# A Mamba-2 scan core rebuilt inside a hybrid encoder kernel: the step size goes into the exponent, the states come first

## The chip, the cores and the metric

The kernel runs on one core of a Trainium2 chip. The number compared is the device time of one execution in microseconds (us). Three runs of the kernel before took 1838.66, 1839.87 and 1843.01 us; their median, 1839.87 us, is the time that the prediction is for. Differences under 0.2% (3.7 us) count as no change.

The engines are TensorE (PE in the profile, with its weight loads as PEld), VectorE (DVE), ScalarE (ACT), GpSimd (POOL) and SyncE (SP, which issues the DMAs). Each engine works through its own list of instructions in a fixed order and waits at an instruction whose inputs or output buffer are not ready. The accumulators that PE writes lie in PSUM banks; everything else is in SBUF.

## The reference

Two layers on a sequence of 512 tokens of width 1024. Each layer normalises, projects, runs four groups of heads (a bidirectional Mamba-2 scan, a bidirectional RWKV-7 scan, differential attention, grouped-query attention), projects back and adds. The change lies in the first group alone:

```python
def _ssd(x, dt, A, bm, cm):                       # chunks of 128 tokens
    xdt = chunk(x * dt[..., None])
    a_cum = jnp.cumsum(dt * A, axis=-1)
    scores = einsum("bclhn,bcshn->bhcls", cm, bm) * exp(segsum(a))      # within a chunk
    y_diag = einsum("bhcls,bcshp->bclhp", scores, xdt)
    decay_states = exp(a_cum[..., -1:] - a_cum)
    states = einsum("bclhn,bclhp->bchpn", bm, xdt * decay_states)       # one per chunk
    ...                                                                 # carried from chunk to chunk
    y_off = einsum("bclhn,bchpn->bclhp", cm, states) * exp(a_cum)
    return y_diag + y_off
...
y = ssd(forward) + flip(ssd(backward)) + xs * d_skip
y = rms_norm_in_2_groups(y * silu(z))
```

There are 8 heads of 64 channels in 2 groups of 4; the state has 128 entries. Both directions are needed for every head.

## The kernel before

A layer has these stages: RWKV with the attention heads woven in, the Mamba-2 part (`ssd`), and the output projection (`mix` matmuls). Projections run as three matmuls for one product: each weight tile `wf` is split into a rounded part `whi` (ACT) and a rest `wlo` (POOL, or DVE for some output weights), so that every block of projection matmuls needs one ACT and one POOL instruction before it.

`ssd` first makes the step sizes (64 rows of 512 tokens: 8 heads forward, 8 heads backward at row 32) and their cumulative sums `ac` on DVE, with two exponentials and a logarithm on ACT. Three row tiles, `ac` (tile `se`), the step size `dt` (tile `sdt`) and the decay to the end of the chunk times the step size `dec` (tile `su`), are transposed on PE into `colT`, so that a token's value is a column usable as a per-partition scalar. `exT` is the exponential of the first.

Then it works through two groups g of four heads. For each head and direction a matmul `prow` spreads that head's cumulative sums over all partitions; DVE subtracts the column and takes the minimum with a mask `mneg` (four chunks, L811), ACT takes the exponential (L814). Two passes of DVE over both directions multiply by the step size and add (L819, L820), a third multiplies by the scores `gT` (L823), and PE makes `yd` from the result `mt` and the inputs `xs`; ACT moves `yd` into `y` for two heads at a time (L830). ACT also takes from each `prow` the decay of a whole chunk, `etot` (L807). After the four heads come the states: `xd` (POOL, L840), the matmul `stp`, the carried states `H` (POOL L847, DVE L850), the matmul `po` for the contribution of the carried states, `of` (DVE L861) and its addition to `y` (POOL L864), then the skip term `sk` (POOL L867) added by DVE (L869). At last `y` is gated with `zs` (L872), squared on ACT (`jk`), normalised into `zs` (L881), and later turned by PE (`ytr`) for the output projection.

Meanwhile PE is fed with other work. A filler holds generators of projection matmuls: for group 0 the projections of group 1 (96 `pjc` and 96 `pjt`, all of which must be out before group 1 starts), for group 1 the output projection's first half, which takes the contributions `kt` 4 to 15 in turn. Calls such as `fill(F_S3)` let it emit a set amount. Contributions 4 to 7 come from RWKV and are used as they are loaded; those from 8 on must first be transposed by PE (`ytr`) into a PSUM bank with the tag `pj`, of which there are two. The banks with the tag `g`, also two, serve `prow`, `yd`, `stp`, `po`, `pxt` and `pg`. After emission a list scheduler with a cost model of its own sets the order on each engine; it may move instructions ahead of others on the same engine.

Of the kernel before, what the change touches and what calls it, by code (L numbers as in the profile page):

```python
# [19 lines left out]
L = 512  # L20
# [55 lines left out]
def trunk(ctx: ExitStack, tc: tile.TileContext, x_in, win, wwd, wdt, wout, w2a, cols, rows, sscal, consts, out, dbg=None,  # L76
# [602 lines left out]
    def ssd(i, lay, ps, sp, op, yA, fill, more):  # L679
# [50 lines left out]
                            op=ALU.subtract)  # L730
        S.activation(dec, dec, AF.Exp)
        V.tensor_tensor(dec, dec, dt, op=ALU.mult)
        colT = sp.tile([128, 3, 4, 64], F32, tag="colT", name="colT")
        for n, src in enumerate((ac, dt, dec)):
            pcx = ps.tile([128, 4, 64], F32, tag="g", name="pcx")
# [55 lines left out]
        for g in range(2):  # L791
# [39 lines left out]

            H = [[None] * 4, [None] * 4]
            for step in range(3):
                stp = ps.tile([128, 2, 256], F32, tag="g", name="stp")
                for d in range(2):
                    ch = step if d == 0 else 3 - step
                    nx = ch + 1 if d == 0 else ch - 1
                    row = 32 * d + 4 * g
                    xd = sp.tile([128, 4, 64], F32, tag="xd", name="xd", bufs=2)
                    G.tensor_tensor(xd, xs[:, ch, :].rearrange("p (h v) -> p h v", h=4),  # L840
                                    colT[:, 2, ch, row:row + 4].unsqueeze(2).to_broadcast([128, 4, 64]), op=ALU.mult)
                    mm(stp[:, d, :], bt[:, ch, :], xd.rearrange("p h v -> p (h v)"), True, True)
                    hn = sp.tile([128, 256], F32, tag=f"H{d}{step}", name="H")
                    if step == 0:
                        V.tensor_copy(hn, stp[:, d, :])
                    else:
                        G.tensor_tensor(hn.rearrange("p (h v) -> p h v", h=4),  # L847
                                        H[d][ch].rearrange("p (h v) -> p h v", h=4),
                                        etot[:, d, ch, :].unsqueeze(2).to_broadcast([128, 4, 64]), op=ALU.mult)
                        V.tensor_tensor(hn, hn, stp[:, d, :], op=ALU.add)  # L850
                    H[d][nx] = hn
                fill(F_S3)
            for ch in range(4):
                po = ps.tile([128, 2, 256], F32, tag="g", name="po")
                ds = [d for d in range(2) if H[d][ch] is not None]
                for d in ds:
                    mm(po[:, d, :], cv[6 + g][:, ch * 128:ch * 128 + 128], H[d][ch], True, True)
                of = sp.tile([128, 2, 256], F32, tag="of", name="of", bufs=2)
                for d in ds:
                    row = 32 * d + 4 * g  # L860
                    V.tensor_tensor(of[:, d, :].rearrange("p (h v) -> p h v", h=4),  # L861
                                    po[:, d, :].rearrange("p (h v) -> p h v", h=4),
                                    exT[:, ch, row:row + 4].unsqueeze(2).to_broadcast([128, 4, 64]), op=ALU.mult)
                    G.tensor_tensor(y[:, ch, :], y[:, ch, :], of[:, d, :], op=ALU.add)  # L864
                fill(F_S4)
                sk = sp.tile([128, 256], F32, tag="sk", name="sk", bufs=2)
# [464 lines left out]
def _consts():  # L1331
# [17 lines left out]
    c[:, C_MNEG + 128:C_MNEG + 256] = np.where(p[:, None] >= p[None, :], 0.0, -1e30)  # L1349
# [102 lines left out]
```

## Time and profile before

| | |
|---|---|
| profiled execution | 1827.76 us, of it span 1826.0 us |
| PE busy | 1596.3 us (87%) |
| PEld busy | 1321.8 us (72%) |
| DVE busy | 1088.5 us (60%) |
| ACT busy | 826.5 us (45%) |
| POOL busy | 695.9 us (38%) |
| mean granted TensorE clock | 0.929 of full speed |
| `ssd` of the first layer, from its first matmul to the end of `y` | about 676 to 845 us |
| `ssd` of the second layer | about 1583 to 1754 us |

A row of the timeline gives the start, the duration, the engine, the line, what is written and read, and in brackets how long the engine had stood idle and what released it. A matmul's duration overlaps that of the next; what PE can do is read from the distance of starts.

### The profile page before, as it was taken

What the parts mean: (1) busy time and instruction counts of PE and PEld (TensorE: products, weight loads), DVE (VectorE), ACT (ScalarE), POOL (GpSimd) and SP (SyncE); (2) the same over time, 40 slices, a digit from 0 to 9 for tenths busy, and PEclk for the clock granted to TensorE, in tenths of its full rate; (3) what the DMA queues carried; (4) which work ended last, traced back from release to release, by engine and by line L of the source; (5) the groups of instructions that cost most, each with busy time, mean ns of one, the idle gap of its engine ahead of it and who ended that gap; (6) DMA issues with size and microseconds to landing.
All of it is one profiled execution on the core that took longest, in us unless ns stands there. A gap on an engine that the chain in (4) does not pass through costs nothing. (4 is left out here: it accounts for less than half of the span.)

```text
span 1826.0 us, 36868 instructions
## 1 busy us (share of the span) xinstructions
PE 1596.3 (87%) x15232; PEld 1321.8 (72%) x15232; DVE 1088.5 (60%) x2130; ACT 826.5 (45%) x1602; POOL 695.9 (38%) x708
## 2 busy tenths in 40 slices
PE   6888889879899898988887998898788989989888
PEld 6677767757788776766775787677567777768666
DVE  3577576575555437885245865755755554288852
ACT  4645336417345335543346453454272453454431
POOL 4543234242424234543455422343333332245333
PEclk9889989989999998999998899899898999989899
DMA  4110001011101014122321100111110110131223
GB/s 148 64 50 32 29 33 59 14 67 35 42 19 62 28 53 138 59 94 81 127 99 54 53 20 29 34 59 36 44 42 31 36 58 22 54 130 53 87 86 116
DMA packets 57512, 108.50 MB, mean 59 GB/s; under 512 B 6784, under 2 KB 8704, under 8 KB 57344
## 3 DMA queue, kind: packets, MB, share of 16 engines
q1 hardware_dynamic: 57344, 106.15, 17.4%
q8 instruction: 119, 1.95, 0.4%
q14 instruction: 49, 0.40, 0.1%
HBM read 95.64 MB, written 10.49 MB: 58 GB/s over the span
## 5 line engine op out<-in xcount | busy, mean ns | idle before, releaser
L145 POOL TENSOR_TENSOR wlo<-wf,whi 128x512 fp32r<-128x512 f32 x228 | 319.6, 1408 | 423.8 <-ACT whi L144 391.3
L82 PE MATMUL pjt<-whi,hhi 128*128 128x256 f32 x960 | 291.3, 303 | 3.7 <-ACT raw L270 1.7
L82 PE MATMUL pjt<-wlo,hhi 128*128 128x256 f32 x960 | 284.5, 297 | 0.8 <-POOL wlo L145 0.8
L82 PE MATMUL pjt<-whi,hlo 128*128 128x256 f32 x960 | 285.2, 297 | 0.0
L144 ACT ACTIVATE whi<-wf 128x512 fp32r<-128x512 f32 x228 | 142.1, 627 | 226.3 <-PE pjt L82 122.6
L82 PEld LDWEIGHTS pjt<-whi,hhi 128*128 128x128 f32 x960 | 191.8, 200 | 15.6 <-issue 7.3
L82 PEld LDWEIGHTS pjt<-whi,hlo 128*128 128x128 f32 x960 | 191.9, 200 | 6.1 <-issue 5.0
L82 PEld LDWEIGHTS pjt<-wlo,hhi 128*128 128x128 f32 x960 | 191.2, 199 | 5.2 <-issue 3.3
L82 PE MATMUL pjc<-hhi,whi 128*128 128x512 f32 x384 | 160.0, 417 | 16.9 <-ACT craw L751 10.7
L82 PE MATMUL pjc<-hhi,wlo 128*128 128x512 f32 x384 | 157.4, 410 | 3.5 <-POOL wlo L145 3.5
L82 PE MATMUL pjc<-hlo,whi 128*128 128x512 f32 x384 | 156.5, 407 | 0.0
L82 PE MATMUL mix<-whi,ylo 128*128 128x512 f32 x256 | 105.8, 413 | 5.5 <-DVE ylo L1234 5.5
L892 ACT ACTIVATE p<-sc,nm 128x512 f32<-128x512 f32 x96 | 65.6, 685 | 89.0 <-DVE nm L889 81.8
L82 PE MATMUL mix<-wlo,yhi 128*128 128x512 f32 x256 | 103.7, 405 | 0.0
L82 PEld LDWEIGHTS pjc<-hhi,whi 128*128 128x128 f32 x384 | 75.0, 195 | 39.5 <-ACT craw L751 12.4
L82 PE MATMUL mix<-whi,yhi 128*128 128x512 f32 x256 | 99.8, 412 | 4.0 <-ACT yhi L1233 4.0
L889 DVE TENSOR_REDUCE nm<-sc 128x1 f32<-128x512 f32 x96 | 64.5, 689 | 63.2 <-PE sc L82 63.1
L82 PE MATMUL pa<-AR,BK 64*64 64x128 f32 x1024 | 66.3, 341 | 37.7 <-DVE AT L450 37.5
L82 PEld LDWEIGHTS pjc<-hhi,wlo 128*128 128x128 f32 x384 | 75.2, 196 | 23.3 <-POOL wlo L145 5.6
L82 PE MATMUL sc<-qT,qT 64*128 64x512 f32 (+1 forms) x256 | 86.4, 478 | 3.8 <-ACT y L1050 1.8
L82 PEld LDWEIGHTS pa<-AR,BK 64*64 64x64 f32 x1024 | 52.8, 171 | 48.7 <-DVE AT L450 42.4
L82 PEld LDWEIGHTS pjc<-hlo,whi 128*128 128x128 f32 x384 | 75.6, 197 | 15.0 <-issue 0.7
(360 smaller groups left out, 3645.4 us busy)
## 6 DMA issues: line engine op xcount, KB each, us to landing
wf<-in_win_dram SPq DMA_DIRECT2D x224, 256.0 KB, 3.0
wf<-in_wout_dram SPq DMA_DIRECT2D x64, 256.0 KB, 2.7
y<-y_dram SPq DMA_DIRECT2D x24, 256.0 KB, 3.4
xt<-in_x_dram SPq DMA_DIRECT2D x8, 512.0 KB, 4.2
y_dram<-y SPq DMA_DIRECT2D x16, 256.0 KB, 3.3
y_dram<-rs SPq DMA_DIRECT2D x8, 256.0 KB, 2.8
x_dram<-t SPq DMA_DIRECT2D x8, 256.0 KB, 2.1
xt<-x_dram SPq DMA_DIRECT2D x4, 512.0 KB, 4.0
```

The costliest lines, as they stand in the source:

```text
L82: PE.matmul(o, lhsT, rhs, start=start, stop=stop, skip_group_check=skip)
L144: S.activation(hi, wf, AF.Copy)
L145: G.tensor_tensor(lo, wf, hi.bitcast(F32), op=ALU.subtract)
L889: V.tensor_reduce(nm, sc, axis=AX, op=ALU.max, negate=True)
L892: S.activation(p, sc, AF.Exp, bias=nm, accum_out=sm)
```

## The change

The step size is no longer a factor on the 128x128 blocks. Its logarithm is taken once per layer in the row layout (after a maximum with 1e-37) and subtracted from the cumulative sum, so that the transposed column already holds both; the minimum with the mask and the exponential then give decay times step size at once. The mask now holds +1e30 where the block is kept. The decays of whole chunks come from one small matmul `pe` per layer instead of 16 small exponentials. In each group the states and the skip term come first: POOL writes the skip term straight into `y`, adds the carried part to it, and only then the four heads follow, whose `yd` is added to `y` by DVE from the bank. For group 1 `yd` lies in a bank with the tag `pj`.

```diff
         V.tensor_tensor(dec, dec, dt, op=ALU.mult)
+        V.tensor_scalar(dt, dt, 1e-37, None, op0=ALU.max)
+        S.activation(dt, dt, AF.Ln)
+        V.tensor_tensor(dt, ac, dt, op=ALU.subtract)
         colT = sp.tile([128, 3, 4, 64], F32, tag="colT", name="colT")
...
+        ends = sp.tile([128, 4, 16], F32, tag="ends", name="ends")
+        for d in range(2):
+            V.tensor_tensor(ends[:, :, 8 * d:8 * d + 8], ac4[:, :, 127 * (1 - d):128 - 127 * d].to_broadcast([128, 4, 8]),
+                            selE.bitcast(F32)[:, 8 * d:8 * d + 8].unsqueeze(1).to_broadcast([128, 4, 8]), op=ALU.mult)
+        pe = ps.tile([128, 4, 16], F32, tag="g", name="pe")
+        mm(pe, one.to_broadcast([128, 128]), ends, True, True)
+        S.activation(etot, pe, AF.Exp)
+        V.tensor_scalar(dh, rws[:, R_D:R_D + 8], 0.5, None, op0=ALU.mult)
...
+            H = [[None] * 4, [None] * 4]          # states: moved ahead of the heads, text as before
+            for step in range(3):
...
+            for ch in range(4):
+                for d in ds:
+                    mm(po[:, d, :], cv[6 + g][:, ch * 128:ch * 128 + 128], H[d][ch], True, True)
+                G.tensor_tensor(heads(y[:, ch, :]), heads(xs[:, ch, :]),
+                                dh[:, 4 * g:4 * g + 4].unsqueeze(2).to_broadcast([128, 4, 64]), op=ALU.mult)
+                of = sp.tile([128, 2, 256], F32, tag="of", name="of", bufs=2)
+                for d in ds:
+                    row = 32 * d + 4 * g
+                    V.tensor_tensor(heads(of[:, d, :]), heads(po[:, d, :]),
+                                    exT[:, ch, row:row + 4].unsqueeze(2).to_broadcast([128, 4, 64]), op=ALU.mult)
+                    G.tensor_tensor(y[:, ch, :], y[:, ch, :], of[:, d, :], op=ALU.add)
+                fill(F_S4)
             for h in range(4):
                 for d in range(2):
                     mm(pr, selE[:, ri:ri + 1].to_broadcast([128, 128]), acs, True, True)
-                    S.activation(etot[:, d, :, h:h + 1], p4[:, :, 127:128] if d == 0 else p4[:, :, 0:1], AF.Exp)
                     for ch in range(4):
-                        V.scalar_tensor_tensor(ar[:, ch, :], p4[:, ch, :], colT[:, 0, ch, row:row + 1],
+                        V.scalar_tensor_tensor(ar[:, ch, :], p4[:, ch, :], colT[:, 1, ch, row:row + 1],
                                                mneg[:, d * 128:d * 128 + 128],
                                                op0=ALU.subtract, op1=ALU.min)
                     S.activation(ar, ar, AF.Exp)
-                for ch in range(4):
-                    V.tensor_scalar(ex[0][:, ch, :], ex[0][:, ch, :], colT[:, 1, ch, row:row + 1], None, op0=ALU.mult)
-                    V.scalar_tensor_tensor(ex[1][:, ch, :], ex[1][:, ch, :], colT[:, 1, ch, row + 32:row + 33],
-                                           ex[0][:, ch, :], op0=ALU.mult, op1=ALU.add)
-                V.tensor_tensor(mt, ex[1], gT, op=ALU.mult)
+                V.tensor_tensor(mt, ex[0], ex[1], op=ALU.add)
+                V.tensor_tensor(mt, mt, gT, op=ALU.mult)
                 if h % 2 == 0:
-                    yd = ps.tile([128, 4, 2, 64], F32, tag="g", name="yd")
+                    yd = ps.tile([128, 4, 2, 64], F32, tag="pj" if g else "g", name="yd")
                 if h % 2 == 1:
-                    S.activation(y[:, :, (h - 1) * 64:(h + 1) * 64], yd.rearrange("p c h v -> p c (h v)"), AF.Copy)
+                    V.tensor_tensor(yh, yd.rearrange("p c h v -> p c (h v)"), yh, op=ALU.add)
...
-                G.tensor_tensor(sk.rearrange("p (h v) -> p h v", h=4), xs[:, ch, :].rearrange("p (h v) -> p h v", h=4),
-                                rws[:, R_D + 4 * g:R_D + 4 * g + 4].unsqueeze(2).to_broadcast([128, 4, 64]), op=ALU.mult)
-                V.scalar_tensor_tensor(y[:, ch, :], sk, 0.5, y[:, ch, :], op0=ALU.mult, op1=ALU.add)
...
-    c[:, C_MNEG:C_MNEG + 128] = np.where(p[:, None] <= p[None, :], 0.0, -1e30)
+    c[:, C_MNEG:C_MNEG + 128] = np.where(p[:, None] <= p[None, :], 1e30, -1e30)
```

The order on the engines changes in the Mamba-2 part of both layers only. Three places of it, in the first layer:

ACT, where the columns `colT` are made, before (`su` is the decay row, `craw` empties a projection bank of PE):

```order
L731 ACTIVATE su<-su 64x512
L1233 ACTIVATE yhi<-y 128x512
L144 ACTIVATE whi<-wf 128x512
L738 ACTIVATE colT<-pcx 128x256
L144 ACTIVATE whi<-wf 128x512
L758 ACTIVATE cv<-cacc 128x512
L751 ACTIVATE craw<-pjc 128x512
```

and now:

```order
L731 ACTIVATE su<-su 64x512
L1244 ACTIVATE yhi<-y 128x512
L144 ACTIVATE whi<-wf 128x512
L735 ACT_TABLE_LOAD
L735 ACTIVATE sdt<-sdt 64x512
L775 ACT_TABLE_LOAD
L775 ACTIVATE cv<-cacc 128x512
L742 ACTIVATE colT<-pcx 128x256 x2
L768 ACTIVATE craw<-pjc 128x512
```

The logarithm with a table load on either side now stands ahead of `craw`, one `colT` has moved behind it, and one `whi` has gone from ahead of `craw` to a place further down.

POOL, at the start of group 0, before (`xd` feeds the states, `sk` is the skip term):

```order
L145 TENSOR_TENSOR wlo<-wf,whi 128x512 x2
L840 TENSOR_TENSOR xd<-xs,colT 128x256 x2
L867 TENSOR_TENSOR sk<-xs,srow 128x256 x2
L145 TENSOR_TENSOR wlo<-wf,whi 128x512 x7
L749 MEMSET craw 128x2
L750 MEMSET craw 128x2
L145 TENSOR_TENSOR wlo<-wf,whi 128x512
L840 TENSOR_TENSOR xd<-xs,colT 128x256
L847 TENSOR_TENSOR H<-H,etot 128x256
```

and now:

```order
L145 TENSOR_TENSOR wlo<-wf,whi 128x512 x2
L824 TENSOR_TENSOR xd<-xs,colT 128x256 x2
L843 TENSOR_TENSOR y<-xs,dh 128x256 x4
L824 TENSOR_TENSOR xd<-xs,colT 128x256
L832 TENSOR_TENSOR H<-H,etot 128x256
L824 TENSOR_TENSOR xd<-xs,colT 128x256 x2
L832 TENSOR_TENSOR H<-H,etot 128x256 x2
L824 TENSOR_TENSOR xd<-xs,colT 128x256
L832 TENSOR_TENSOR H<-H,etot 128x256
L145 TENSOR_TENSOR wlo<-wf,whi 128x512
L850 TENSOR_TENSOR y<-y,of 128x256 x6
L145 TENSOR_TENSOR wlo<-wf,whi 128x512 x4
```

The chain of the states, which was spread behind the weight splits of the heads, is now one block at the start of the group, with the four skip products inside it.

PE, in group 1 around the second head's `yd`, before:

```order
L82 MATMUL yd<-xs,mt 128x64 x4
L82 MATMUL mix<-wlo,yhi 128x512
L82 MATMUL mix<-whi,ylo 128x512
L82 MATMUL mix<-wlo,yhi 128x512
L82 MATMUL mix<-whi,ylo 128x512
L82 MATMUL prow<-acs,cr 128x512
L82 MATMUL mix<-wlo,yhi 128x512
```

(12 more `mix`, 8 `ytr` and 3 `mix` follow before the third head's `yd`), and now:

```order
L82 MATMUL mix<-whi,ylo 128x512
L82 MATMUL mix<-wlo,yhi 128x512
L82 MATMUL yd<-xs,mt 128x64 x4
L82 MATMUL prow<-acs,cr 128x512 x2
L82 MATMUL yd<-xs,mt 128x64 x4
L1239 MATMUL ytr<-cst,y 128x128 x4
L82 MATMUL mix<-whi,yhi 128x512 x4
```

Between the second and the third head's `yd` there is now no `mix`: 48 of them, which is four contributions, stand ahead of it, and the first `ytr` stands behind the third `yd`.

## Rows read from the trace of the kernel before

**Rows 1.** The page, part 1: busy time (share) xinstructions of PE.

```profile
PE 1596.3 (87%) x15232; PEld 1321.8 (72%) x15232; DVE 1088.5 (60%) x2130; ACT 826.5 (45%) x1602; POOL 695.9 (38%) x708
```

**Rows 2.** Busy time by stretch: length, engines, granted clock, DMA share, GB/s.

```profile
697.00:734.00 37.00, 30.72 (x178) 25.75 (x178) 31.93 (x35) 21.54 (x38) 20.20 (x22) 0.86 0.43 145
734.00:796.00 62.00, 53.32 (x293) 44.38 (x292) 53.30 (x116) 26.90 (x57) 34.65 (x39) 0.97 0.18 57
796.00:842.00 46.00, 43.58 (x217) 34.27 (x215) 35.76 (x99) 17.87 (x37) 16.44 (x21) 1.00 0.28 86
842.00:866.00 24.00, 20.52 (x82) 15.69 (x81) 13.22 (x20) 9.83 (x26) 5.66 (x5) 0.86 0.32 110
1641.00:1703.00 62.00, 53.36 (x288) 44.43 (x287) 52.81 (x114) 26.71 (x57) 34.28 (x38) 0.93 0.17 55
1749.00:1775.00 26.00, 20.44 (x90) 15.73 (x88) 14.22 (x22) 10.16 (x26) 7.03 (x7) 0.93 0.32 102
```

**Rows 3.** Waits of PE, 697 to 734: total, times, longest.

```profile
PE pjc L82 <- ACT craw L751: 4.3, 1, 4.3
```

**Rows 4.** Waits of PE, 734 to 796, group 0 of the first layer.

```profile
PE pxt L777 <- ACT xs L778: 5.1, 1, 5.1
PE pg L82 <- DVE cv L759: 1.3, 1, 1.3
```

**Rows 5.** Waits of PE, 842 to 866, behind group 1 of the first layer.

```profile
PE mix L82 <- DVE ylo L1234: 2.8, 1, 2.8
```

**Rows 6.** Groups of DVE instructions, 734 to 796: busy, mean ns, idle before.

```profile
L811 DVE SCALAR_TENSOR_TENSOR ar<-prow,colT,mneg 128x128 f32<-128x128 f32 x32 | 8.9, 343 | 4.6 <-ACT etot L807 4.6
L820 DVE SCALAR_TENSOR_TENSOR ar<-ar,colT 128x128 f32<-128x128 f32 x16 | 5.9, 431 | 0.2 <-ACT ar L814 0.2
L819 DVE TENSOR_SCALAR ar<-ar,colT 128x128 f32<-128x128 f32 x16 | 5.5, 399 | 0.8 <-ACT ar L814 0.8
L869 DVE SCALAR_TENSOR_TENSOR y<-sk,y 128x256 f32<-128x256 f32 x4 | 4.2, 1060 | 2.1 <-POOL y L864 2.1
L823 DVE TENSOR_TENSOR mt<-ar,gT 128x512 f32<-128x512 f32 x4 | 2.7, 684 | 0.0
```

**Rows 7.** Groups of PE instructions, 734 to 796.

```profile
L82 PE MATMUL stp<-xd,bt 128*128 128x256 f32 x12 | 3.7, 405 | 0.8 <-POOL xd L840 0.7
L82 PE MATMUL po<-H,cv 128*128 128x256 f32 x12 | 3.0, 389 | 0.0
```

**Rows 8.** Tile colT: duration ns min/median/max, first and last start.

```profile
L840 POOL TENSOR_TENSOR xd<-xs,colT x24: 606/613/1058, 733.1 to 1741.0; 128x256 f32<-128x256 f32 x24
```

**Rows 9.** Tile H.

```profile
L847 POOL TENSOR_TENSOR H<-H,etot x16: 612/988/1059, 767.2 to 1741.9; 128x256 f32<-128x256 f32 x16
```

**Rows 10.** Tile y.

```profile
L872 DVE SCALAR_TENSOR_TENSOR y<-y,zs x4: 1212/1220/1225, 786.4 to 1752.7; 128x1024 f32<-128x1024 f32 x4
```

**Rows 11.** Timeline of PE, 790 to 797.

```profile
790.96 1.11 PE L777 MATMUL pxt<-cst,cv 128*128 128x128 f32 x4 [5.09 <-ACT xs L778]
...
795.05 1.13 PE L82 MATMUL pg<-cv 128*128 128x128 f32 x8 [1.27 <-DVE cv L759]
...
796.25 0.39 PE L82 MATMUL mix<-wlo,yhi 128*128 128x512 f32 x1
796.48 0.39 PE L82 MATMUL mix<-whi,yhi 128*128 128x512 f32 x1
```

**Rows 12.** Timeline of ACT, 695 to 719.

```profile
695.85 1.28 ACT L707 ACT_TABLE_LOAD   x1
697.14 0.63 ACT L707 ACTIVATE sl<-su 64x512 f32<-64x512 f32 x1
...
718.10 0.60 ACT L751 ACTIVATE craw<-pjc 128x512 f32<-128x512 f32 x1 [0.22 <-PE pjc L82]
```

**Rows 13.** Groups of DVE instructions, 703 to 734.

```profile
L723 DVE TENSOR_SCALAR sdt<-sdt 64x512 f32<-64x512 f32 x1 | 1.3, 1317 | 0.0
L732 DVE TENSOR_TENSOR su<-su,sdt 64x512 f32<-64x512 f32 x1 | 0.7, 675 | 0.0
```

More of the change, by code (lines that the diff above doesn't have):

```diff
@@ L740, in ssd @@
         S.activation(exT, colT[:, 0], AF.Exp)
+        ends = sp.tile([128, 4, 16], F32, tag="ends", name="ends")
+        ac4 = acs.bitcast(F32).rearrange("p (c t) -> p c t", c=4)
+        for d in range(2):
[3 more added lines that the diff above has]
+        mm(pe, one.to_broadcast([128, 128]), ends, True, True)
+        etot = sp.tile([128, 4, 16], F32, tag="etot", name="etot")
+        S.activation(etot, pe, AF.Exp)
+        dh = sp.tile([128, 8], F32, tag="dh", name="dh")
+        V.tensor_scalar(dh, rws[:, R_D:R_D + 8], 0.5, None, op0=ALU.mult)
         gr = [{}, {}]
@@ L795, in ssd @@
             cv, zs, xs, bt, gT = (gr[g][n] for n in ("cv", "zs", "xs", "bt", "gT"))
-            etot = sp.tile([128, 2, 4, 4], F32, tag="etot", name="etot")
+            heads = lambda t: t.rearrange("p (h v) -> p h v", h=4)
             y = sp.tile([128, 4, 256], F32, tag="y", name="y")
+            H = [[None] * 4, [None] * 4]
+            for step in range(3):
+                stp = ps.tile([128, 2, 256], F32, tag="g", name="stp")
+                for d in range(2):
+                    ch = step if d == 0 else 3 - step
+                    nx = ch + 1 if d == 0 else ch - 1
+                    row = 32 * d + 4 * g
+                    xd = sp.tile([128, 4, 64], F32, tag="xd", name="xd", bufs=2)
+                    G.tensor_tensor(xd, heads(xs[:, ch, :]),
+                                    colT[:, 2, ch, row:row + 4].unsqueeze(2).to_broadcast([128, 4, 64]), op=ALU.mult)
+                    mm(stp[:, d, :], bt[:, ch, :], xd.rearrange("p h v -> p (h v)"), True, True)
+                    hn = sp.tile([128, 256], F32, tag=f"H{d}{step}", name="H")
+                    if step == 0:
+                        V.tensor_copy(hn, stp[:, d, :])
+                    else:
+                        er = 8 * d + 4 * g
+                        G.tensor_tensor(heads(hn), heads(H[d][ch]),
+                                        etot[:, ch, er:er + 4].unsqueeze(2).to_broadcast([128, 4, 64]), op=ALU.mult)
+                        V.tensor_tensor(hn, hn, stp[:, d, :], op=ALU.add)
+                    H[d][nx] = hn
+                fill(F_S3)
@@ new lines, in ssd @@
+            for ch in range(4):
+                po = ps.tile([128, 2, 256], F32, tag="g", name="po")
+                ds = [d for d in range(2) if H[d][ch] is not None]
+                for d in ds:
[4 more added lines that the diff above has]
+                for d in ds:
+                    row = 32 * d + 4 * g
+                    V.tensor_tensor(heads(of[:, d, :]), heads(po[:, d, :]),
+                                    exT[:, ch, row:row + 4].unsqueeze(2).to_broadcast([128, 4, 64]), op=ALU.mult)
+                    G.tensor_tensor(y[:, ch, :], y[:, ch, :], of[:, d, :], op=ALU.add)
+                fill(F_S4)
@@ L829, in ssd @@
                 if h % 2 == 1:
-                    S.activation(y[:, :, (h - 1) * 64:(h + 1) * 64], yd.rearrange("p c h v -> p c (h v)"), AF.Copy)
[L832 to L866, printed above, removed]
-                G.tensor_tensor(sk.rearrange("p (h v) -> p h v", h=4), xs[:, ch, :].rearrange("p (h v) -> p h v", h=4),
-                                rws[:, R_D + 4 * g:R_D + 4 * g + 4].unsqueeze(2).to_broadcast([128, 4, 64]), op=ALU.mult)
-                V.scalar_tensor_tensor(y[:, ch, :], sk, 0.5, y[:, ch, :], op0=ALU.mult, op1=ALU.add)
@@ L870, in ssd @@
+                    yh = y[:, :, (h - 1) * 64:(h + 1) * 64]
+                    V.tensor_tensor(yh, yd.rearrange("p c h v -> p c (h v)"), yh, op=ALU.add)
             tap("ssdy", y, lambda a: a[:, g * 256:g * 256 + 256].rearrange("(c p) v -> p c v", p=128))
@@ L1347, in _consts @@
     c[:, C_I64:C_I64 + 64] = (s[:, None] == np.arange(64)[None, :])
-    c[:, C_MNEG:C_MNEG + 128] = np.where(p[:, None] <= p[None, :], 0.0, -1e30)
-    c[:, C_MNEG + 128:C_MNEG + 256] = np.where(p[:, None] >= p[None, :], 0.0, -1e30)
+    c[:, C_MNEG:C_MNEG + 128] = np.where(p[:, None] <= p[None, :], 1e30, -1e30)
+    c[:, C_MNEG + 128:C_MNEG + 256] = np.where(p[:, None] >= p[None, :], 1e30, -1e30)
     n = np.arange(512)
```

1 line of the change is left out of this document (removed).

## The prediction

> **What bounds the kernel now.** I read the busy times first: PE is busy 87% of the span, and no other engine comes near [rows 1]. The three-way projection matmuls stay as they are, so the change can only win where PE stands idle. Next come the stretches [rows 2]. PE's idle time is length less busy time: in the first layer 8.7 us of the 62 us of group 0 (734 to 796), 2.4 us of the 46 us of group 1, and 3.5 us of the 24 us behind it; in the second layer 8.6 us for group 0 and 5.6 us behind group 1 (its group 1 repeats the first layer's). Then the waits. In group 0 most of the idle time is one wait of 5.1 us, of `pxt` for ACT's copy `xs`, and 1.3 us of `pg` for DVE [rows 4]. Neither is DVE's arithmetic on the heads: ACT's list has the four squares `jk` ahead of that copy, and these wait until `y` is finished, which takes the states, `po` and the skip term behind the last head. Behind group 1 PE waits 2.8 us for a `ylo` that stands on DVE behind the same kind of `y` [rows 5]. Ahead of the groups it waits 4.3 us for `craw` [rows 3].
>
> Idle time has a second price. A mean granted clock of 0.97 over 62 us is 3.7 us at the half level (1.2 GHz), 0.93 is 8.7 us, 0.86 over 24 us is 6.7 us [rows 2]. It falls behind such long waits. Half of what is left of it after the waits that fall into it is lost: (3.7 - 1.3) / 2 = 1.2 us in group 0 of the first layer, 3.2 us in the second (some 2.3 us of waits taken off), 2.3 us behind group 1 in the first, 1.2 us in the second.
>
> **The change part by part.** *DVE.* Per head and layer, four L819 (0.399 us) and four L820 (0.431 us) go and one whole-tile add comes, taken as L823 (0.684 us): 4 x 0.83 - 0.68 = 2.6 us less; over eight heads 21 us per layer by this stretch. The `sk` additions go (8 x 1.06 us), four additions of `yd` come (0.68 each, from ACT, which had them as copies) [rows 6]. None of this counts by itself: in group 0 DVE was busy 53.3 of 62 us, but so was PE [rows 2], and PE's waits there for `mt` are small change. It counts only as far as it shortens the end of `y`.
>
> *Preamble (+0.8 us a layer).* Ahead of `craw`, which began at 718.10, ACT now has the logarithm and two table loads of 1.28 us [rows 12]; on DVE come a maximum (bounds: nothing if it falls into an idle moment, 1.32 us as L723) and a subtraction (0.68 us as L732) [rows 13], and two tiny products. Following ACT's list from the end of `su`: the logarithm ends some 3.5 us later, `cv` and two `colT` follow, and `craw` starts at about 719. PE meanwhile has 35 `pjc` with no transposes between them and has moved four `pxt` forward, so that it reaches the first `pjt` 0 to 0.5 us late; `pe` costs 0.15 us and the next `whi` about 0.3 us. I take 0.8 us, between 0 and 2.6 us (both loads on PE's path).
>
> The trace prices the load at 1.28 us, and the logarithm behind it starts 0.01 us after its end [rows 12]. The Trainium skill (ScalarE: Activation LUTs, What ACT_TABLE_LOAD costs) adds a drain of about 1.38 us to each switch, 2.66 us in all. By that rule the preamble would be about 2.8 us dearer per layer.
>
> *States first (new waits).* In the new POOL order each group has two `xd`, four skip products, then `xd` and `H` alternating: 14 instructions from the first `xd` to the last `H`. At 0.61 us [rows 8, 9] that is 8.5 us plus one DVE addition, 9.0 us. PE has in that time six `stp` and six `po` (at most 3.7 + 3.0 us busy for both [rows 7], nearer 4.5 us by distance of starts) and 13 projection matmuls at 0.23 us [rows 11], 3.0 us, of which the `po` mostly come after the chain. `stp` number 3 waits for the xd behind the four skip products (2.3 us), the three after it 0.6, 0.35 and 0.65 us: 3.9 us in group 0. In group 1 POOL starts earlier against PE, since `pg` comes later than `xs`: 1.85 us. Before, this cost 0.7 us, as other work lay between. `H` has a median of 0.99 us and `xd` a maximum of 1.06 us [rows 8, 9]; at means of 0.71 and 1.02 us the chain would be 11.2 us, 2.7 us more in each of the four groups. I take 0.61, the median of `xd`, because only PSUM-reading DVE work lies beside the chain now.
>
> The Trainium skill (SBUF — State Buffer, Who interferes with whom) says that a DVE instruction with two SBUF inputs shuts out a GpSimd one that reads SBUF, and that one with at most one SBUF input does not. The spread of `xd` from 0.606 to 1.058 us agrees with it [rows 8]; by that rule the chain runs at 0.61.
>
> *End of group 0.* After the last head there are now one addition (0.68), the gating of 1.22 us [rows 10] and four squares, about 4.5 us, against 46 `pjt` (5.5 us) that PE still has: the 5.1 us wait goes. `pg` still waits for DVE, which has the four `zs` ahead of `cv`: 1.4 us. So group 0: before 8.7 + half clock 1.2 (second layer 8.6 + 3.2); now 3.9 + 1.4 + 1.2 for a fall of the clock behind the states: **-3.4 and -5.3 us**.
>
> *Group 1.* DVE needs per head eight `ar` (8.9 / 4 = 2.2 us), the tail of an exponential (0.6, as `craw`) and two whole-tile passes (1.4): 4.2 us [rows 6, 12]. PE has filler for it until 48 `mix` are used up; the next contribution needs a transpose into a `pj` bank, and `yd` holds one of the two until DVE has added it, the other being taken by the second `yd`. In the new order PE has two `prow` (0.5 us) between the second and third `yd`, against DVE's 4.2 us, of which 0.3 us are done by then: 3.4 us idle, plus 0.65 us for the first `yhi`. With the states' 1.85 us that is 5.9 us, and half clock 1.7 us; before 2.4 us: **+5.2 us** a layer.
>
> *Behind group 1.* `y` ends 2.5 us after the last `yd`, with transposes of two contributions and 24 `mix` at hand; 1.2 us of waits remain. Before: 3.5 + 2.3 and 5.6 + 1.2 us: **-4.6 and -5.6 us**.
>
> Sum: first layer 0.8 - 3.4 + 5.2 - 4.6 = -2.0; second 0.8 - 5.3 + 5.2 - 5.6 = -4.9; together -6.9 us. I take 6, since some of the idle time before is gaps too short to be listed, which will stay. The profiled execution (1827.76 us: 1826.0 and 1.76 around it) would become 1822. It lies 12.1 us under the median of the runs, and I carry the difference over: 1839.9 - 6 = **1834 us**.
>
> **Rivals.** (1) *The state chain on POOL becomes the bound, and the kernel is slower.* Place: the start of each group. Price: at the means of this stretch, 4 x 2.7 = 10.8 us more, and PE's clock falls longer: -6 + 10.8 + 2 gives +7, 1847 us. It cancels the gain at a mean of 0.72 us per instruction and costs 0.2% from 0.78 us. For it: `H` had 0.99 us in the median [rows 9]. Against: that was with two-input DVE passes beside it, which have left this place. Chance 0.22.
> (2) *The preamble eats the gain: no change.* If each of the two loads holds ACT twice its 1.28 us, `craw` comes 2.6 us later, PE stands at the bank, and 2 x 2.6 = 5 us are lost: 1839 us. For it: PE waited 4.3 us for just this copy, and a half clock followed [rows 2, 3]. Against: the load's row ends where the next begins [rows 12]. It is the place where the drain of the ScalarE page would show. Chance 0.17.
> (3) *More gain.* If PE's weights and banks let it take other work between the second and third `yd`, so that group 1 costs about what it did, 2 x 4.5 of its 2 x 5.2 us fall away: -6 - 9 gives 1825 us. For it: DVE has 4 x 2.6 + 4 x 1.06 - 2 x 0.68 = 13 us less in each group. Against: the order is fixed, and nothing ready stands there. Chance 0.13.
>
> **The numbers.** Forecast 0.48, with its own range 1828 to 1840. Range over all: 1823 to 1848. A change under 0.2% (3.7 us, so 1836.2 to 1843.5) can't be told from none. Faster: 0.40 of the forecast's 0.48 and all of (3), 0.53. Same: 0.08 of the forecast and (2), 0.25. Slower: (1), 0.22.
>
> **What would show it.** The `pxt` wait of 5.1 us is gone in both layers and no wait over 2.5 us stands in its place there; `stp` waits for `xd` about 4 us in group 0; PE waits 3 us or more for the third `yd` of group 1; `ylo` behind group 1 costs under 1.5 us. `xd` and `H` at 0.61 us against 0.8 and more decides between the forecast and (1), the start of the first `pjt` behind the `pjc` between it and (2). I am wrong if PE's half clock grows by more than 5 us, which no list of waits gives, or if the waits of group 1 stay at 2.4 us.

## The result: 0.7% slower

The kernel before took 1839.2 us in the median of ten runs, the changed one 1850.1 us (1846.6 to 1854.9). The ratio is 1.0069, with a 95% interval of 1.0042 to 1.0096. The forecast was 1834 us, faster; the time lies outside the range of 1823 to 1848. A later set (e8 below) gave 1.0089 (1.0063 to 1.0115).

The profiled execution of the changed kernel has a span of 1846.6 us, 20.6 us over that of before, which was one of that kernel's fastest. The page, part 1, answers to [rows 1]: DVE has lost 34 us of work, PE is busy 6 us longer.

```profile
PE 1602.5 (87%) x15236; PEld 1326.2 (72%) x15236; DVE 1054.6 (57%) x2020; ACT 822.9 (45%) x1570; POOL 693.1 (38%) x708
```

To find the place, I cut each layer at starts of PE's instructions which both kernels have: the last `pc` ahead of the `pjc`, the first `pjt` behind them, `pg` of group 0, `pg` of group 1, and the end of the output projection (`trp` of the next layer; in the second layer the last matmul). First the first layer of before in these cuts, by the windows (length, busy time of PE, PEld, DVE, ACT, POOL, granted clock, DMA share, GB/s):

```profile
681.00:719.30 38.30, 29.91 (x115) 21.82 (x116) 26.34 (x33) 23.14 (x36) 16.99 (x18) 0.87 0.43 143
719.30:733.10 13.80, 13.80 (x113) 13.24 (x111) 11.47 (x12) 7.55 (x14) 7.31 (x10) 1.00 0.28 95
733.10:795.10 62.00, 53.32 (x293) 44.38 (x291) 52.40 (x114) 27.50 (x58) 34.65 (x40) 0.97 0.19 60
795.10:908.90 113.80, 102.56 (x467) 81.24 (x467) 58.28 (x132) 41.40 (x86) 41.22 (x40) 0.96 0.33 110
```

The changed kernel, the same four stretches:

```profile
685.20:726.20 41.00, 30.12 (x121) 22.47 (x121) 26.51 (x38) 24.93 (x39) 16.44 (x17) 0.83 0.38 124
726.20:740.90 14.70, 13.44 (x110) 12.91 (x108) 12.33 (x12) 8.42 (x17) 8.63 (x10) 1.00 0.34 113
740.90:800.40 59.50, 52.76 (x281) 43.69 (x280) 42.06 (x83) 24.54 (x47) 30.99 (x37) 0.94 0.18 59
800.40:924.10 123.70, 107.56 (x477) 84.41 (x477) 50.44 (x104) 39.81 (x77) 41.96 (x44) 0.96 0.32 103
```

The lengths by themselves tell most: 2.7 us more, 0.9 more, 2.5 less, 9.9 more. One correction: in its group 0 stretch the kernel before had issued 17 `mix` already, the changed one 6. Eleven `mix` at 0.23 us [rows 11] are 2.5 us that change sides. At equal work the first layer is 3.6 us slower ahead of group 0, even in group 0, and 7.4 us slower behind it; the second layer 3.1 slower, 1.4 faster and 5.7 slower. Together that is 11.1 and 7.4 us; the rest of the 20.6 us lies outside the two cuts, in code that is the same in both.

**Ahead of the groups.** DVE, 698 to 702 us of the changed kernel (start, duration, line, operation; in brackets how long DVE stood idle and for whom):

```profile
698.16 0.68 DVE L704 SCALAR_TENSOR_TENSOR se<-xb 64x512 f32<-64x512 f32 x1
701.42 0.17 DVE L757 TENSOR_SCALAR dh<-srow 128x8 f32<-128x8 f32 x1 [2.59 <-DMA srow<-in_rows_dram]
701.50 0.74 DVE L773 SCALAR_TENSOR_TENSOR cacc<-craw,cols,cacc 128x512 f32<-128x512 f32 x1
702.16 0.41 DVE L706 TENSOR_SCALAR su<-se 64x512 f32<-64x512 f32 x1
```

The scheduler has put the tiny product `dh` ahead of the step size's logarithm. It takes 0.17 us, but the row table `srow` that it reads was requested only at 696.41 and took 5.0 us to land. DVE stands for 2.6 us, and with it the scans, `pcx` and all behind them. PE waits 3.9 us for `pcx`'s input, 1.3 before, and further on 1.3 us for `zs`, where before has no wait (before, then twice the changed kernel; total, times, longest):

```profile
PE pcx L737 <- DVE se L718: 1.3, 1, 1.3
PE pcx L741 <- DVE se L718: 3.9, 1, 3.9
PE pjc L82 <- DVE zs L786: 1.3, 1, 1.3
```

**Group 0.** The 5.1 us wait of [rows 4] is gone, as forecast. What PE waits for now, 740.9 to 800.4 (total, times, longest):

```profile
PE yd L82 <- DVE mt L872: 3.1, 4, 1.5
PE stp L82 <- POOL xd L824: 2.3, 1, 2.3
PE pg L82 <- DVE cv L776: 1.0, 1, 1.0
PE prow L82 <- DVE of L848: 0.3, 1, 0.3
```

The `stp` wait is that of the third `stp`; POOL's timeline shows what it stood behind, four skip products between the second and third `xd`:

```profile
741.37 1.18 POOL L824 TENSOR_TENSOR xd<-xs,colT 128x256 f32<-128x256 f32 x2
742.51 2.32 POOL L843 TENSOR_TENSOR y<-xs,dh 128x256 f32<-128x256 f32 x4
744.80 0.60 POOL L824 TENSOR_TENSOR xd<-xs,colT 128x256 f32<-128x256 f32 x1
745.37 0.60 POOL L832 TENSOR_TENSOR H<-H,etot 128x256 f32<-128x256 f32 x1
```

**Group 1.** PE's timeline from its second to its third `yd`:

```profile
822.46 0.40 PE L82 MATMUL mix<-wlo,yhi 128*128 128x512 f32 x1
824.67 1.10 PE L82 MATMUL yd<-xs,mt 128*128 128x64 f32 x8 [1.81 <-DVE mt L872]
826.98 0.47 PE L82 MATMUL prow<-acs,cr 128*128 128x512 f32 x1 [1.20 <-DVE ar L864]
828.01 0.77 PE L82 MATMUL prow<-acs,cr 128*128 128x512 f32 x1 [0.56 <-DVE ar L864]
830.10 1.97 PE L82 MATMUL yd<-xs,mt 128*128 128x64 f32 x8 [1.32 <-DVE mt L872]
831.86 1.06 PE L1239 MATMUL ytr<-cst,y 128*128 128x128 f32 x4
833.61 2.07 PE L82 MATMUL mix<-whi,yhi 128*128 128x512 f32 x4 [0.69 <-ACT yhi L1244]
835.48 0.63 PE L82 MATMUL mix<-whi,ylo 128*128 128x512 f32 x1
835.91 0.63 PE L82 MATMUL mix<-wlo,yhi 128*128 128x512 f32 x1
```

The four heads' `yd` lie in two tiles, the first two heads in one and the others in the next, and each tile takes a `pj` bank. No output projection at all stands between the second and the third `yd`, and no transpose `ytr` before 831.86. DVE had emptied the first tile at 826.6 (its addition starts at 825.89 and takes 0.69 us), but PE's fixed order has the first `ytr` behind the third `yd`; how much is the full bank and how much the order made around it, no run separates. The listed waits are short, but the clock falls to its half level, 1.2 GHz, at 827.8, behind the first two, and stays there until 838.1. The `mix` then come at 0.43 us instead of 0.23 (windows as above):

```profile
822.80:827.80 5.00, 1.64 (x10) 1.15 (x9) 3.99 (x11) 1.12 (x2) 0.00 (x0) 1.00 0.16 54
827.80:838.10 10.30, 8.08 (x24) 6.24 (x25) 5.60 (x14) 2.27 (x4) 0.00 (x0) 0.50 0.09 27
```

Behind group 1 the wait for `ylo` is 0.8 us, 2.8 before [rows 5].

### The profile page after: what moved, and what is told of

Same layout as the page of the kernel before. It is cut to its first block, busy times and chain, and to the rows that moved or that the text cites. A ratio compares the mean times of both kernels' runs of the same rounds, so it can differ in the third digit from the quotient of the medians.

```text
span 1846.6 us, 36753 instructions
## 1 busy us (share of the span) xinstructions
PE 1602.5 (87%) x15236; PEld 1326.2 (72%) x15236; DVE 1054.6 (57%) x2020; ACT 822.9 (45%) x1570; POOL 693.1 (38%) x708
## 5 line engine op out<-in xcount | busy, mean ns | idle before, releaser
L145 POOL TENSOR_TENSOR wlo<-wf,whi 128x512 fp32r<-128x512 f32 x228 | 323.2, 1424 | 422.8 <-ACT whi L144 390.7
L144 ACT ACTIVATE whi<-wf 128x512 fp32r<-128x512 f32 x228 | 142.0, 627 | 236.6 <-PE pjt L82 118.1
L82 PEld LDWEIGHTS pjc<-hhi,whi 128*128 128x128 f32 x384 | 76.6, 200 | 43.1 <-ACT craw L768 13.5
L900 DVE TENSOR_REDUCE nm<-sc 128x1 f32<-128x512 f32 x96 | 64.3, 687 | 66.1 <-PE sc L82 65.9
L1253 POOL TENSOR_TENSOR wlo<-wf,whi 128x512 fp32r<-128x512 f32 x32 | 43.8, 1372 | 153.2 <-ACT whi L1252 149.7
L82 PE MATMUL pa<-AR,BK 64*64 64x128 f32 x1024 | 65.3, 337 | 39.4 <-DVE AT L450 39.4
L1252 ACT ACTIVATE whi<-wf 128x512 fp32r<-128x512 f32 x64 | 40.3, 631 | 120.5 <-PE mix L82 90.8
```

What stands on the lines that cost most here:

```text
L82: PE.matmul(o, lhsT, rhs, start=start, stop=stop, skip_group_check=skip)
L144: S.activation(hi, wf, AF.Copy)
L145: G.tensor_tensor(lo, wf, hi.bitcast(F32), op=ALU.subtract)
L900: V.tensor_reduce(nm, sc, axis=AX, op=ALU.max, negate=True)
L1252: S.activation(hi, wf, AF.Copy)
L1253: (V if kt % 2 else G).tensor_tensor(lo, wf, hi.bitcast(F32), op=ALU.subtract)
```

## The experiments

The theory after this first reading (A): three separate losses, namely `yd` in `pj` (largest), `dh` waiting for a DMA, the skip products in POOL's chain. Rivals: the logarithm and its table loads (B, D), DVE's own work per head in group 1 (C), and waits that would only move to another place (E and others). Times are medians, with the ratio to the kernel before in the same set; a set's median of before is 1834.2 (e1 to e4), 1833.7 (e5 to e8) or 1835.4 us (e9 to e11). Each of the three sets ran on a chip of its own, so between sets the ratios are the better measure.

| run | median us | ratio, 95% interval |
|---|---|---|
| e1 logarithm alone | 1833.2 | 0.9982 (0.9954 to 1.0011) |
| e2 order and bank alone | 1866.4 | 1.0155 (1.0107 to 1.0202) |
| e3 changed, yd in g | 1829.8 | 0.9972 (0.9950 to 0.9995) |
| e4 changed, no logarithm | 1846.4 | 1.0058 (1.0030 to 1.0085) |
| e5 e3 and dh late | 1821.1 | 0.9929 (0.9901 to 0.9956) |
| e6 e3 and skip on DVE | 1821.6 | 0.9932 (0.9907 to 0.9957) |
| e7 all three | 1817.5 | 0.9912 (0.9880 to 0.9943) |
| e8 changed once more | 1851.2 | 1.0089 (1.0063 to 1.0115) |
| e9 before, yd in pj | 1852.7 | 1.0089 (1.0058 to 1.0120) |
| e10 changed, dh late | 1844.0 | 1.0049 (1.0030 to 1.0068) |
| e11 e7 and early logarithm | 1814.3 | 0.9894 (0.9857 to 0.9932) |

The four stretches of each profiled run in us, first layer / second layer, and the `mix` between the four `yd` of group 1 (first layer). The stretch to the first `pjt` is called the preamble below. A stretch is read from one execution; e8, the changed kernel in another set, repeats each within 0.4 us:

| run | to first `pjt` | to `pg` | group 0 | group 1 and behind | `mix` between `yd` |
|---|---|---|---|---|---|
| before | 38.2 / 40.1 | 13.8 / 13.8 | 62.0 / 62.0 | 113.8 / 116.0 | 23, 20, 22 |
| changed | 41.0 / 42.2 | 14.7 / 14.7 | 59.5 / 58.1 | 123.8 / 124.3 | 10, 0, 11 |
| e1 | 39.1 / 39.9 | 14.9 / 14.9 | 57.4 / 57.5 | 119.3 / 118.4 | 21, 23, 20 |
| e2 | 41.2 / 43.5 | 13.8 / 13.8 | 62.1 / 64.3 | 129.3 / 125.1 | 0, 0, 7 |
| e3 | 41.4 / 41.7 | 14.7 / 14.7 | 59.6 / 59.5 | 113.1 / 112.3 | 21, 18, 20 |
| e4 | 41.1 / 41.5 | 13.8 / 13.8 | 57.0 / 57.0 | 124.1 / 123.2 | 10, 0, 11 |
| e5 | 38.3 / 39.4 | 14.7 / 14.7 | 58.3 / 57.5 | 113.8 / 113.2 | 21, 18, 20 |
| e6 | 41.2 / 41.7 | 14.7 / 14.7 | 56.2 / 56.1 | 112.3 / 110.9 | 21, 17, 20 |
| e7 | 38.3 / 39.4 | 14.7 / 14.7 | 56.1 / 57.4 | 112.1 / 110.8 | 21, 17, 20 |
| e8 | 41.4 / 42.2 | 14.7 / 14.7 | 59.5 / 58.0 | 124.0 / 124.3 | 10, 0, 11 |
| e9 | 38.0 / 40.2 | 13.8 / 13.8 | 62.0 / 62.0 | 126.3 / 126.0 | 6, 0, 4 |
| e10 | 38.2 / 38.9 | 14.7 / 14.7 | 58.2 / 58.2 | 124.7 / 124.3 | 10, 0, 11 |
| e11 | 39.7 / 42.2 | 13.6 / 13.6 | 55.7 / 55.8 | 112.3 / 110.9 | 21, 17, 20 |

(Before and e9 have 17 `mix` in group 0, e2 21, e1 4, the others 6.) The one-line edits go through the list scheduler too, so the order of other instructions can move with them; the stretches tell where. The ratio of e8, 1.0089, is a little above the 1.006 to 1.008 expected of it, which its interval holds.

**e1, the logarithm alone.** The kernel before with three edits, states and skip last as they were:

```diff
+        V.tensor_scalar(dt, dt, 1e-37, None, op0=ALU.max)
+        S.activation(dt, dt, AF.Ln)
+        V.tensor_tensor(dt, ac, dt, op=ALU.subtract)
...
-                        V.scalar_tensor_tensor(ar[:, ch, :], p4[:, ch, :], colT[:, 0, ch, row:row + 1],
+                        V.scalar_tensor_tensor(ar[:, ch, :], p4[:, ch, :], colT[:, 1, ch, row:row + 1],
...
-                V.tensor_tensor(mt, ex[1], gT, op=ALU.mult)
+                V.tensor_tensor(mt, ex[0], ex[1], op=ALU.add)
+                V.tensor_tensor(mt, mt, gT, op=ALU.mult)
```

(The two passes per chunk go, the mask is that of the change.)

> The kernel before with the logarithm of the step size in the exponent alone; states, skip and the copies of yd stay where they were. Theory A (the loss is made by the order of states and skip and by the bank of yd, the logarithm itself costs about 2 us a layer ahead of the groups): 2 us lost in the preamble, 3 to 5 us won at the end of each group 0 since DVE has 2.6 us less per head; 1833 to 1838 us against 1839. Theory B (the logarithm with its table loads is the loss): 1845 us or more.

No loss: B falls. The preamble is 0.9 us longer and 0.2 shorter, and the stretch to `pg` 1.1 us longer in each layer. But little gain either, and less in group 0 than A's 3 to 5 us: at equal work 1.6 and 1.5 us. The wait for `xs` at the end of group 0 is halved, not gone, since the states still stand there, and group 1 has a new wait for a contribution's rounded part, whose cause stays open (lines: total, times, longest; group 0, then group 1 and behind):

```profile
PE pxt L781 <- ACT xs L782: 2.5, 1, 2.5
...
PE mix L82 <- ACT yhi L1233: 4.7, 4, 3.9
```

**e2, order and bank alone.** The changed kernel with the old two passes per chunk and without the logarithm:

```diff
-                V.tensor_tensor(mt, ex[0], ex[1], op=ALU.add)
-                V.tensor_tensor(mt, mt, gT, op=ALU.mult)
+                for ch in range(4):
+                    V.tensor_scalar(ex[0][:, ch, :], ex[0][:, ch, :], colT[:, 1, ch, row:row + 1], None, op0=ALU.mult)
...
+                V.tensor_tensor(mt, ex[1], gT, op=ALU.mult)
```

> The changed kernel without the logarithm: the old two passes per head and chunk multiply by the step size again; states and skip first, yd added from its bank. Theory A: states in group 0 cost 7 us a layer, the bank of yd 9, and DVE has 2.6 us more per head where PE already waits for it: 1855 to 1865 us. Theory B: about 1840 us or less.

As A has it, and 1 us beyond its range: the order with its bank is the loss, and DVE's shorter heads hid part of it. The preamble is as late without the logarithm (41.2 and 43.5 us) as with it; the stretch to `pg` is back at 13.8 us.

**e3, `yd` back in `g`.**

```diff
-                    yd = ps.tile([128, 4, 2, 64], F32, tag="pj" if g else "g", name="yd")
+                    yd = ps.tile([128, 4, 2, 64], F32, tag="g", name="yd")
```

> The changed kernel with yd of group 1 back in the banks g, so that the contributions' transposes find both pj banks free. Theory A (the bank starves PE of output projection work between the second and the last head): the waits for mt and prow of 4.9 us and the half clock behind them go, 7 to 9 us a layer, 1832 to 1838 us. Rival C (DVE's 4.2 us per head bound group 1 whatever the bank): under 3 us in all, 1847 us or more.

One word gives back 20 us of the median, more than A's 12 to 18 (the sets differ; by the stretches it is 10.7 and 12.0 us, and ahead of group 1 no stretch moves by more than 1.4). C falls: DVE has the same work per head, and no `yd` of group 1 waits. The second `yd` of that kernel and what leads to it:

```profile
815.64 0.40 PE L82 MATMUL prow<-acs,cr 128*128 128x512 f32 x1
815.87 0.39 PE L82 MATMUL mix<-wlo,yhi 128*128 128x512 f32 x1
816.10 1.03 PE L1239 MATMUL ytr<-cst,y 128*128 128x128 f32 x8
817.38 0.50 PE L82 MATMUL mix<-whi,yhi 128*128 128x512 f32 x1 [0.25 <-ACT yhi L1244]
817.72 0.40 PE L82 MATMUL prow<-acs,cr 128*128 128x512 f32 x1
...
820.73 1.00 PE L82 MATMUL yd<-xs,mt 128*128 128x64 f32 x8
```

The transposes of two contributions (816.10) stand between the heads again. The window of group 1 and behind shows both halves of the gain:

```profile
794.20:907.30 113.10, 102.56 (x477) 81.60 (x477) 49.53 (x104) 39.30 (x77) 42.19 (x44) 1.00 0.34 112
```

Idle time is 10.5 us against 16.1, and PE is busy 5.0 us less for the same matmuls, at a clock of 1.00 instead of 0.96.

**e9, the same edit in the kernel before, the other way.**

```diff
-                    yd = ps.tile([128, 4, 2, 64], F32, tag="g", name="yd")
+                    yd = ps.tile([128, 4, 2, 64], F32, tag="pj" if g else "g", name="yd")
```

> The kernel before with one edit: yd of group 1 in a bank pj instead of g. Theory A (the bank alone starves group 1 of output projection work, in whatever order the rest stands): 8 to 11 us lost per layer, 1850 to 1858 us, with the waits and the half clock behind the first yd of group 1. Rival C2 (the bank costs only together with states first, where yd is emptied by DVE; ACT's copy empties it at once here): under 4 us in all, 1838 us or less.

A, within its range: 17 us lost by this edit alone, and the ratio, 1.0089, is that of the whole change in e8. It needs neither the new order nor the addition from the bank. Of the 12.5 us that the last stretch of the first layer is longer, some 2.6 are not the bank's, by an estimate: the clock had fallen at 795.3, in the wait for `xs` ahead of group 1, and stayed at half until 805.5 (5.3 us of the stretch, all but 0.02 with PE busy), in before only until 793.8. PE's timeline in group 1:

```profile
816.00 1.97 PE L82 MATMUL yd<-xs,mt 128*128 128x64 f32 x8 [2.77 <-DVE mt L823]
817.73 1.20 PE L82 MATMUL prow<-acs,cr 128*128 128x512 f32 x2
821.86 1.97 PE L82 MATMUL yd<-xs,mt 128*128 128x64 f32 x8 [2.93 <-DVE mt L823]
```

**e4, no logarithm.**

```diff
-        S.activation(dt, dt, AF.Ln)
+        S.activation(dt, dt, AF.Copy)
```

> The changed kernel with the logarithm replaced by a plain copy on ACT (the logarithm is left out of the computation, so the exponent is not the reference's), which takes the two table loads per layer away and nothing else. Theory A (the loads hold craw and the copies of colT back, PE reaches the first pjt 2.2 and 1.4 us late): 3 to 4 us less than the changed kernel, 1846 us. Rival D (the lateness comes from the DVE maximum and subtraction and the place of the transposes, the loads are hidden): under 1.5 us.

The times leave the size open: the median is 3.7 and 4.8 us under the changed kernel's two, the ratio 2.0 and 5.7 us, and the intervals overlap. The stretches sum to 3.0 and 3.8 us less in the two layers, more than A's 3 to 4 in all. The place is not A's: the preamble stays at 41.1 and 41.5 us. What goes is PE's wait of 1.3 us for `zs` ahead of `pg`, and 2.5 and 1.1 us of group 0, whose clock is now whole, though the `stp` wait behind the skip products (2.0 us) is still there:

```profile
726.00:739.80 13.80, 13.80 (x113) 13.23 (x112) 11.44 (x13) 7.45 (x14) 7.55 (x10) 1.00 0.38 128
739.80:796.80 57.00, 50.05 (x281) 41.05 (x281) 42.02 (x82) 24.74 (x47) 30.53 (x36) 1.00 0.18 61
```

Of D, the half holds that says the preamble is late for another reason than the loads; its number, under 1.5 us, is excluded by the stretches and not by the times. The `zs` wait is the logarithm's in any case: the stretch to `pg` is 13.8 us in both kernels of the new order that lack it (e2, e4).

**e5 and e10, `dh` late,** with `yd` in `g` and in the changed kernel:

```diff
-        V.tensor_scalar(dh, rws[:, R_D:R_D + 8], 0.5, None, op0=ALU.mult)
+        V.tensor_scalar(dh, exT[:, 0, 0:8], 0.0, 0.5, op0=ALU.mult, op1=ALU.add)
+        V.tensor_tensor(dh, dh, rws[:, R_D:R_D + 8], op=ALU.mult)
```

> The changed kernel with yd of group 1 in the banks g (the run with yd in g before), and the tiny product dh = D / 2 made to wait for exT, so that it stands behind the scans on DVE. Theory A2 (in the changed kernel dh stands ahead of the step size's logarithm on DVE and waits 2.6 us there for the DMA of srow; this holds the scan, pcx and all that follows): the preamble falls from 41.4 and 41.7 us to 39 and 39.5, 4 to 5 us less in all, about 1825 us. Rival: PE would only wait longer for craw or zs instead: under 1.5 us.

> The changed kernel with one edit: the tiny product dh waits for exT, so that it stands behind the scans on DVE (yd stays in pj). Theory A2: the preamble falls by 3.1 and 2.3 us, 5 to 8 us less than the changed kernel, about 1844 us. Rival: with group 1 still starved, what is won ahead is lost at the bank: under 2 us.

Both as A2 (theory A for `dh`): the preamble is back at 38.3 and 39.4 us (38.2 and 38.9 in e10), the length of before, logarithm and all. In e5 the gain is larger than A2's 4 to 5 us, 8 us by the ratios. In e10 the interval alone would not exclude the rival, but the stretches sum to 3.2 us less in each layer. e10 has DVE's list without the gap:

```profile
695.65 0.68 DVE L704 SCALAR_TENSOR_TENSOR se<-xb 64x512 f32<-64x512 f32 x1
696.25 0.74 DVE L774 SCALAR_TENSOR_TENSOR cacc<-craw,cols,cacc 128x512 f32<-128x512 f32 x1
697.02 0.42 DVE L706 TENSOR_SCALAR su<-se 64x512 f32<-64x512 f32 x1
```

**e6 and e7, the skip products on DVE,** on top of e3, without and with `dh` late:

```diff
-                G.tensor_tensor(heads(y[:, ch, :]), heads(xs[:, ch, :]),
+                V.tensor_tensor(heads(y[:, ch, :]), heads(xs[:, ch, :]),
```

> The changed kernel with yd of group 1 in the banks g, and the four skip products of each group on DVE instead of POOL. Theory A (they stand in the POOL chain of the states, and stp waits 2.2 us for the xd behind them, four times, with a half clock after it): the waits of stp for xd fall under 0.7 us, 8 to 10 us less in all, about 1820 us. Rival E (the chain xd, stp, H has the same length, PE waits for H or po instead; or DVE instructions with two SBUF inputs beside POOL stretch xd to 1 us): under 3 us.

> All three: yd of group 1 in the banks g, dh late, skip products on DVE. Theory A: both gains add, 1816 us. Rival: where either gain is taken back by another wait, 1823 us or more.

The median of e6 is 8 us under that of e3 (7 by the ratios), by the stretches 3.4 us in each group 0 and about 1 behind it; the long `stp` wait is gone (0.9 us in three waits are left in group 0, A had under 0.7). Half of E showed: the `xd` beside the DVE products were slower, three in 2.31 us, where the changed kernel had 0.60 us apiece:

```profile
740.80 2.31 POOL L824 TENSOR_TENSOR xd<-xs,colT 128x256 f32<-128x256 f32 x3
743.80 0.61 POOL L832 TENSOR_TENSOR H<-H,etot 128x256 f32<-128x256 f32 x1 [0.69 <-DVE H L829]
```

It cost 0.5 us and did not decide. The rule that the prediction cited (the Trainium skill, SBUF — State Buffer, Who interferes with whom) agrees with these 0.77 us; the prediction left out that the page excepts DVE's two-port modes. e7 lies between: 1817.5 us, 3.6 and 4.0 under e5 and e6, with overlapping intervals; A's 1816 and the rival's 1823 bracket it, nearer to A. By the stretches the two gains are 7.1 and 9.2 us alone and 13.5 together, so most of each adds.

**e11, the logarithm early,** on top of e7:

```diff
+        V.tensor_scalar(lg, dt, 0.125, 1e-37, op0=ALU.mult, op1=ALU.max)
+        S.activation(lg, lg, AF.Ln)
...
-        V.tensor_scalar(dt, dt, 1e-37, None, op0=ALU.max)
-        S.activation(dt, dt, AF.Ln)
-        V.tensor_tensor(dt, ac, dt, op=ALU.subtract)
+        V.tensor_tensor(dt, ac, lg, op=ALU.subtract)
```

> The three mends together (yd in g, dh late, skip products on DVE), and the logarithm taken directly from the step size, one DVE instruction earlier than before the scans, so that ACT has it in a moment in which it waits. Theory A (the logarithm with its table loads makes zs 1.3 us late in each layer, and a half clock with it, as the run without the logarithm showed): the wait of pjc for zs goes, 2.5 to 4 us less than with the three mends, about 1814 us. Rival: an own maximum on DVE ahead of the scans, and still two table loads, cost as much there: no difference from 1817 us.

The median is A's 1814, but the intervals of e7 and e11 overlap, and the stretches of the two sum to the same 221.3 and 222.4 us: the `zs` wait and some of group 0 went (1.1 us, and 0.4 and 1.6), and the preamble took 1.4 and 2.8 us for it, with a new wait of `pcx` for `sdt` of 1.2 and 1.6 us. The rival has it: no difference that the runs show. Either version beats both kernels, by 0.9 and 1.1% against before.

## Why the prediction was wrong

**The step that failed** is the size of the term for group 1. The mechanism was named: the next contribution needs a transpose into a `pj` bank, and `yd` holds one and then both. But I let it begin behind the second `yd` and end with the third, put the waits at 5.9 us and the half clock at 1.7 us, and took the half clock behind group 1 as saved. The `mix` counts show the shortage from the first `yd` to the last (10, 0, 11 for 23, 20, 22). The waits of group 1 came out at 8.2 us (`stp` 2.6 for 1.85 forecast, `yd` and `prow` 4.9 for 3.4, the first `yhi` 0.7). With the stretch behind it I had forecast +0.6 and -0.4 us; measured at equal work are +7.4 and +5.7. PE's idle time and its clock have about equal parts in the miss: idle time +4.9 and +2.3 us against +1.2 and -0.9 forecast, PE's work at equal work +2.5 and +3.5 us longer against -0.6 and +0.5. Against e3, where the clock stays whole, PE's work of this stretch lasts 5.0 and 7.0 us longer for the same matmuls. e3 and e9 put 10 to 12 us a layer on this one tag.

Over both layers the sum missed by 12.9 us here, 7.3 in group 0 and 5.1 in the preamble and up to `pg`. So it is luck that e3, without the tag, meets the forecast (its 0.9972 is 1834 us at the 1839.2 of before): the forecast has +5.2 us a layer for group 1 in it, and rival (3), which takes 4.5 of them out, said 1825. What e3 saves there it loses in the other two places.

**The preamble** (+0.8, bounds 0 to 2.6) came out at +2.7 and +2.2 us, and 0.9 more ahead of `pg`. The table loads, to which I gave the bounds, did not hold the preamble: e4 has it as late without them. The logarithm with its loads cost the 0.9 ahead of `pg`, by e2 and e4. I had also taken the wrong copy for the price. The wait of 4.3 us in [rows 3] is for an earlier `craw`, which began at 702.53; behind the one at 718.10 PE runs without a gap. In the changed kernel, too, PE waits for the earlier one (4.7 us) and not for the one behind the logarithm.

```profile
702.53 0.58 ACT L751 ACTIVATE craw<-pjc 128x512 f32<-128x512 f32 x1
703.16 0.79 PE L82 MATMUL pjc<-hhi,whi 128*128 128x512 f32 x1 [4.35 <-ACT craw L751]
```

The price of the preamble stood in an instruction that my list of additions to DVE held, if at all, among the tiny products at no price: `dh` takes 0.17 us but waits 2.6 us for a DMA on an engine that works in order. e5 and e10 give 2.3 to 3.3 us a layer for it. Rival (2) had the place and nearly the size, with a cause that did not happen, and the wait that it cites is that of the earlier `craw`. The drain of the Trainium skill (ScalarE: Activation LUTs, What ACT_TABLE_LOAD costs) does not show: in the changed kernel the logarithm follows its load of 1.28 us at once.

```profile
720.02 1.28 ACT L735 ACT_TABLE_LOAD   x1
721.32 0.63 ACT L735 ACTIVATE sdt<-sdt 64x512 f32<-64x512 f32 x1
```

**Group 0** (-3.4 and -5.3) was 0.0 and -1.4 at equal work. Right: the `xs` wait goes; `pg` waits 1.0 us (1.4 forecast); `xd` and `H` take 0.61 us in the median; the wait is behind the four skip products (2.26 us, 2.3 forecast). Too high: the waits of the later `stp` (1.6 us forecast, none listed). Missed: 3.1 us of `yd` waits for `mt` where there were 1.1 (3.0 and 3.1 in e3, e4 and e6 too; their cause stays open), and in the first layer 1.7 us more of half clock (62 x 0.03 against 59.5 x 0.06). With the skip products on DVE (e6) the group comes 3.4 us lower in each layer. That this is the forecast of the first layer is chance: the forecast had the products on POOL.

**Behind group 1** the `ylo` wait went from 2.8 to 0.8 us (1.2 forecast), but in the two stretches together, idle time and clock both grew.

**The rivals.** (1) gave the right side and nearly the time, 1847 us, for the wrong reason: POOL's chain ran at 0.61 us, not 0.71 and 1.02. Its place cost 7 to 8 us, by the four instructions in front of it and not by their duration. (3) did not happen. My last sentence named the sign that came, a half clock that grows by more than 5 us: over the eight stretches PE is at the half level for 66 us, 50 before.

## What to carry to other kernels

A bank's tag is a resource of whoever else draws on it: before moving an accumulator to another tag, list what is fed through that tag and count the filler work that is left between two uses. An instruction that takes next to no time can still carry a wait (here 0.17 us and 2.6); in an in-order list, price each added one by when its inputs arrive, DMAs above all. And an idle PE can cost twice, by the wait and by the clock behind it, so compare the length of equal work in both kernels stretch by stretch, not the sums of listed waits.

## What was not expected of the hardware

I had looked for a half clock only at long waits: in the kernel before it began at 701.6 and 790.4, inside the waits of 4.3 and 5.1 us of [rows 3] and [rows 4]. In group 1 of the changed kernel PE waited 1.8 and 1.2 us and stood in a third wait of 0.6 us when the clock fell at 827.8; 1.3 and 0.7 us followed. None of these is long, and the `mix` behind them came at 0.43 us instead of 0.23. Against e3 the lower clock cost 5 us in this stretch of the first layer, about as much as the idle time that e3 removed (5.6 us). In the second layer it cost 7 us, but 3.4 us of the half clock there (granted clock 0.50 from 1718.7 to 1722.1) lie ahead of the first `yd`, behind an `stp` wait of 2.2 us. The same wait in the first layer, and both in e3, left the clock at 1.00. So a listed wait alone does not tell whether the clock will fall.
